# Hybrid decoder layer on one core: the second branch's merge gates made as four seven-product pairs ahead of the recurrence, the attention branch's products moved between its heads

## Chip, core and metric

The program runs on one NeuronCore of one Trainium2 chip, as a single launch. The metric is the device time of one execution in microseconds (us); lower is better. All data are float32. Every large product is made on the tensor engine (PE) from two halves of each operand, a rounded high part and a low remainder, with three matmuls (high by high, high by low, low by high).

## The reference, cut to what matters

One layer over 512 tokens of width 1024: a SwiGLU feed-forward block, a merge of two token mixers, and a second feed-forward block. The change lies in the merge.

```python
u = rms_norm(h, mix_norm_pre[l])
proj = u @ w_in[l]
q, k, v, xr, yr, gl = jnp.split(proj, splits, axis=-1)
...
attn = jnp.einsum('gbsh,gbshe->bshe', alpha, jnp.stack(outs, axis=0).astype(jnp.float32))
attn_d = attn.astype(x.dtype).reshape(B, S, ATTN_OUT_WIDTH) @ w_attn_branch[l]

rec = rg_lru_branch(xr, conv_w[l], conv_b[l], lru_w_x[l], lru_b_x[l],
                    lru_w_a[l], lru_b_a[l], lru_a_param[l]) * jax.nn.gelu(yr)
rec_d = rec @ w_rec_branch[l]

gates = jax.nn.sigmoid(gl).reshape(B, S, N_BRANCHES, D_MODEL)
merged = gates[:, :, 0] * attn_d + gates[:, :, 1] * rec_d
h = h + rms_norm(merged @ w_out[l], mix_norm_post[l])
```

`rg_lru_branch` is a width-4 causal convolution, two gate products per head of 256 channels (four heads), and a linear scan over the 512 tokens.

## The kernel before

Activations stand with the 1024 channels on eight tiles of 128 partitions and the 512 tokens along the row. One "tile" of a product below is 128 output channels by 512 tokens. The code is recorded in program order, and a scheduler then fixes one order of instructions for each engine from priorities (`fetch` and `w_forms` raise the work on weights by 100, PSUM evacuations by 200). On the chip each engine runs its list strictly in that order and waits where an operand or a buffer is not there.

Two ways of making a product matter.

- The plain way, `gemm` (lines L279 to L281 through `mm3`): 24 matmuls of 512 columns for a tile with 1024 input channels, 12 for the attention branch with its 512.
- The seven-product way, `seven` (L639 to L641): two output tiles at once, as a two-by-two block product with seven instead of eight sub-products. Each is 12 matmuls of 256 columns, so a pair is 84 of them. Sums of weight blocks (`w_forms`) and of activation blocks (`forms_of`, names p1 to p7) are formed beforehand.

Weights come as one stream from HBM on SP's queue (`raw_of`, L210), are split into high and low parts by `split` (ACT copies the high part, L264, DVE subtracts the low one, L265), and land in four buffers of 1024 columns (`w8`) or two of 512 (`w4`).

The stretch around the change runs so on PE:

1. the value products, among them `seven512`, which makes two groups of values by seven products (L711 to L713) in the order p1, p2, p6, p7, p4, p5, p3. The activation sums p7 and p5 go into buffers of their own from `big`. The weight blocks u0 come twice into one buffer, `c`, a half of the tile `room`; the other half of it is `first_v`, which sixteen small DMAs on POOL's queue copy elsewhere (L1179);
2. attention for four heads, with the q and k products as twelve pairs between them;
3. four pairs for the first branch's gates (columns 52 to 59 of the stream), with sigmoids into `facc` (L1370, L1371);
4. the eight attention-branch tiles, each multiplied into `facc` by DVE (L1379);
5. the recurrence, a loop over four heads. For head hd it makes two tiles of `branch` (evacuated by DVE, L1443), two of `conv` for the next head (evacuated by ACT, L1427, then the convolution on DVE, L1431), the head's four gate products (`gates_of`, 24 matmuls that read `rec`), and then `recur`, a chain of ACT and DVE work with no PE in it: sigmoid (L1459), tanh (L1470), exp (L1472), a rescale (L1474), then on DVE L1475 to L1477, ACT's square root (L1481), DVE's L1487, L1488, the scan L1489, the product with the gelu branch L1490 and a split into `rec` (L264, L265). Behind `recur` come the second branch's gate tiles that `GATE1` assigns to that head, 0, 2, 2 and 4 of them, made the plain way with a sigmoid out of PSUM (L1505);
6. the eight recurrent-branch tiles, 24 matmuls each, which read all eight tiles of `rec` in order: the last six matmuls of each need the two tiles of the last head.

PSUM has eight banks; in the loop products rotate over four of them and the gate products have the other four. A bank is written again when its earlier content has been read. `h`, needed after stage 6, is fetched back between stages 3 and 4 (L1375).

Of the kernel before, what the change touches and what calls it, by code (L numbers as in the profile page):

```python
# [16 lines left out]
P = 128  # L17
# [23 lines left out]
CB = 6  # L41
GATE1 = ((), (0, 1), (2, 3), (4, 5, 6, 7))

# [25 lines left out]
def stream_plan():  # L69
# [30 lines left out]
    for h in range(NH):  # L100
        qk(h)
    for c in range(0, KC, 2):
        plan.append((("pair", 52 + c, 53 + c), 2048))
    for m in range(KC):
        plan.append((("attn", m), 512))
    for h in range(-1, NH):
        if h >= 0:
            for c in (2 * h, 2 * h + 1):
                plan.append((("in", 44 + c), 1024))
            plan.append((("lru", h), 1024))  # L110
        if h + 1 < NH:
            for c in (2 * h + 2, 2 * h + 3):
                plan.append((("in", 36 + c), 1024))
        if h < 0:
            continue
        for c in GATE1[h]:
            plan.append((("in", 60 + c), 1024))
    for m in range(KC):
# [31 lines left out]
def hybrid_layer(ctx: ExitStack, tc: tile.TileContext, xT: bass.AP, xN: bass.AP, wst: bass.AP,  # L150
# [86 lines left out]
    def big(shape, dt=F32R):  # L237
        return bpool.tile(shape, dt, name="big", tag="b")
# [281 lines left out]

    def forms_of(x, his, los, pool, copied):

# [41 lines left out]
        def fourth():  # L564
            form("p5", big([P, 2, 2, T]), d[1])

# [580 lines left out]
    with ExitStack() as mx:  # L1147
# [66 lines left out]
        vq = [apool.tile([P, T], F32, name="qk", tag="qk", bufs=QKB) for _ in range(4)]  # L1214
        seven512(wbig[0], room[:, 4:8, :].rearrange("q k t -> q (k t)"), vq, v_form, vbank, vy, vz, v_made, v_done)
# [3 lines left out]
        order = [("pair",) + p for ps in pairs for p in ps] + [("pair", 52 + c, 53 + c) for c in range(0, KC, 2)]  # L1219
        forms = {order[0]: w_forms(order[0])}  # L1220

# [144 lines left out]
        for c in range(0, KC, 2):  # L1366
# [3 lines left out]
            ACT.activation(facc[:, c, :], g, AF.Sigmoid)  # L1370
            ACT.activation(facc[:, c + 1, :], u, AF.Sigmoid, scale=-1.0)  # L1371
        apool_cm.__exit__(None, None, None)
        new_h()
        for b in range(4):
            nc.gpsimd.dma_start(hb(b), kept_m[b])  # L1375
        for c in range(KC):
            ps = acc_ps()
            gemm(ps, fetch(("attn", c)), attn)
            DVE.tensor_mul(facc[:, c, :], ps, facc[:, c, :])  # L1379

    with ExitStack() as mx:
        rpool = mx.enter_context(tc.tile_pool(name="rec", bufs=1))
        rec_t = rpool.tile([P, 16, T], F32R, name="rec")
# [111 lines left out]
        for hd in range(NH):  # L1495
# [169 lines left out]
```

## Time and profile before

| | |
|---|---|
| median of three executions | 1230.32 us (1229.68 to 1231.6) |
| the profiled execution | 1229.78 us, of which the span from first to last instruction is 1228.0 us |
| PE busy in the span | 1213.7 us, 99% |
| ACT busy, DVE busy | 740.6 us, 961.2 us |
| granted TensorE clock | 0.998 |
| attention-branch tiles on PE | 615.11 to 636.89 us from the span's start |
| loop over the heads on PE | 636.89 to 791.79 us |
| recurrent-branch tiles on PE | 791.79 to 835.31 us |

Times inside the span are counted from its start. A row of the timeline gives start, duration, engine, line, operation, what is written and read, and in brackets the idle time of the engine before it with what ended it. A PE row's duration is longer than the distance to the next one, since matmuls overlap: the price of a matmul is the distance between starts.

### The profile page before, as it was taken

The page shows a single profiled execution, that of the slowest core. Times are in us where ns is not written, and L with a number is a line of the kernel's source. Part 1 is how long each engine was busy: PE and PEld are TensorE (multiplying, and loading weights), DVE is VectorE, ACT ScalarE, POOL GpSimd, SP SyncE. Part 2 cuts the span into 40 slices and gives each one's busy share as a digit, 9 for nine tenths or more (in the row PEclk, how much of TensorE's full clock was granted, in tenths as well). Part 3 has the DMA queues.
Part 4 walks back from the last instruction along what each step waited for, and adds up shares of the span by engine and source line. Part 5 has one row for each costly group of instructions (what it writes and reads, how often), then busy time and mean ns, then how long its engine had stood idle before and what let it go on. Part 6 is the DMA issues. An engine that isn't in the chain of part 4 may idle for free.

```text
span 1228.0 us, 18986 instructions
## 1 busy us (share of the span) xinstructions
PE 1213.7 (99%) x7556; PEld 1094.4 (89%) x7556; DVE 961.2 (78%) x1504; ACT 740.6 (60%) x1229; POOL 75.6 (6%) x123
## 2 busy tenths in 40 slices
PE   9999999999999999999999999999999999999997
PEld 8898989999878999999988878888899999999996
DVE  7998778988579888888566878655788887979864
ACT  6566665655556564666545878734566665656452
POOL 0001111100102000000000000000110010101000
PEclk9999999999999999999999999999999999999999
DMA  6336646464725322222252222324463555455441
GB/s 245 137 104 172 170 110 175 142 164 119 258 103 166 115 91 91 78 78 104 85 190 73 99 103 69 133 77 166 147 197 104 152 155 153 151 146 159 117 155 69
DMA packets 36025, 163.40 MB, mean 133 GB/s; under 512 B 3936, under 2 KB 7136, under 8 KB 23904
## 3 DMA queue, kind: packets, MB, share of 16 engines
q1 hardware_dynamic: 18288, 107.13, 24.9%
q0 software_dynamic: 17648, 55.06, 17.4%
q8 instruction: 59, 0.97, 0.3%
q14 instruction: 30, 0.25, 0.1%
HBM read 151.69 MB, written 6.29 MB: 129 GB/s over the span
## 4 chain that ended last, share of the span: by engine, by line
PE 84%; DVE 8%; ACT 4%; issue 2%; DMA 2%; SPq 0%; DVEq 0%; ACTq 0%
PE bank L972 9%; PE bank L973 9%; PE bank L974 9%; PE bank L281 5%; PE bank L279 5%; PE bank L280 5%; PE bank L639 4%; PE bank L640 4%; PE bank L641 4%; PE bank L887 4%; PE bank L886 4%; PE bank L888 4%; PE bank L393 3%; PE bank L392 3%; PE bank L394 3%
## 5 line engine op out<-in xcount | busy, mean ns | idle before, releaser
L265 DVE TENSOR_TENSOR w<-raw,w 128x1024 fp32r<-128x1024 f32 (+1 forms) x273 | 295.4, 1093 | 68.7 <-ACT w L264 65.0
L264 ACT ACTIVATE w<-raw 128x1024 fp32r<-128x1024 f32 (+1 forms) x273 | 254.1, 951 | 105.3 <-PE bank L281 50.4
L972 PE MATMUL bank<-big,w 128*128 128x256 f32 x816 | 233.8, 286 | 3.0 <-DVE u L985 1.3
L973 PE MATMUL bank<-big,w 128*128 128x256 f32 x816 | 230.7, 283 | 0.0
L974 PE MATMUL bank<-big,w 128*128 128x256 f32 x816 | 229.4, 283 | 0.0
L972 PEld LDWEIGHTS bank<-big,w 128*128 128x128 f32 x816 | 156.1, 191 | 7.9 <-DVE u L985 2.0
L973 PEld LDWEIGHTS bank<-big,w 128*128 128x128 f32 x816 | 156.2, 191 | 1.6
L974 PEld LDWEIGHTS bank<-big,w 128*128 128x128 f32 x816 | 155.6, 191 | 0.0
L639 PE MATMUL bank<-big,w 128*128 128x256 f32 x320 | 91.8, 287 | 0.0
L640 PE MATMUL bank<-big,w 128*128 128x256 f32 x320 | 91.7, 287 | 0.0
L641 PE MATMUL bank<-big,w 128*128 128x256 f32 x320 | 90.8, 284 | 0.0
L886 PE MATMUL bank<-wd,act 128*128 128x512 f32 x224 | 87.8, 392 | 0.0
L887 PE MATMUL bank<-wd,act 128*128 128x512 f32 x224 | 87.7, 392 | 0.0
L888 PE MATMUL bank<-wd,act 128*128 128x512 f32 x224 | 87.2, 389 | 0.0
L281 PE MATMUL bank<-big,w 128*128 128x512 f32 x192 | 74.8, 390 | 2.1 <-DVE w L265 2.1
L280 PE MATMUL bank<-big,w 128*128 128x512 f32 x192 | 74.7, 389 | 0.0
L279 PE MATMUL bank<-big,w 128*128 128x512 f32 x192 | 74.7, 390 | 0.0
L281 PE MATMUL bank<-act,w 128*128 128x512 f32 (+1 forms) x184 | 64.7, 352 | 0.0
L280 PE MATMUL bank<-act,w 128*128 128x512 f32 (+1 forms) x184 | 64.7, 352 | 0.0
L279 PE MATMUL bank<-act,w 128*128 128x512 f32 (+1 forms) x184 | 64.7, 355 | 0.0
L980 ACT ACTIVATE c<-bank 128x256 f32<-128x256 f32 x70 | 26.6, 381 | 61.2 <-PE bank L974 60.8
L639 PEld LDWEIGHTS bank<-big,w 128*128 128x128 f32 x320 | 61.2, 191 | 1.0
(375 smaller groups left out, 2964.2 us busy)
## 6 DMA issues: line engine op xcount, KB each, us to landing
raw<-in_w SPq DMA_DIRECT2D x90, 1024.0 KB, 4.9
dr<-in_wdn POOLq DMA_DIRECT2D x40, 512.0 KB, 5.4
npair<-in_wdn POOLq DMA_DIRECT2D x32, 512.0 KB, 5.4
big<-act POOLq DMA_DIRECT2D x6, 512.0 KB, 3.2
h<-in_x SPq DMA_DIRECT2D x8, 256.0 KB, 5.2
h<-in_xn POOLq DMA_DIRECT2D x4, 512.0 KB, 5.8
raw<-in_wbig SPq DMA_DIRECT2D x2, 1024.0 KB, 4.7
kept_m<-h POOLq DMA_DIRECT2D x4, 512.0 KB, 2.9
```

Source lines behind the costliest of these rows:

```text
L264: ACT.activation(dh, src, AF.Copy)
L265: DVE.tensor_sub(dl, src, dh.bitcast(F32))
L279: PE.matmul(ps, wh, xh, start=first, stop=False)
L280: PE.matmul(ps, wh, xl, start=False, stop=False)
L281: PE.matmul(ps, wl, xh, start=False, stop=last)
L639: PE.matmul(ps, wh, xh, start=start and k == 0, stop=False, skip_group_check=True)
L640: PE.matmul(ps, wh, xl, start=False, stop=False, skip_group_check=True)
L641: PE.matmul(ps, wl, xh, start=False, stop=k == 3, skip_group_check=True)
L886: PE.matmul(ps, xh, wh, start=start and k == 0, stop=False, skip_group_check=True)
L972: PE.matmul(ps, wh, xh, start=start and k == 0, stop=False, skip_group_check=True)
L973: PE.matmul(ps, wh, xl, start=False, stop=False, skip_group_check=True)
L974: i = PE.matmul(ps, wl, xh, start=False, stop=k == 3, skip_group_check=True)
```

## The change

The second branch's eight gate tiles leave the loop. They are made as four more seven-product pairs directly behind the first branch's four. Their sigmoids are written to a DRAM tile `early` by eight DMAs on POOL's queue, and eight DMAs on the same queue bring them back into `sig` inside the loop. The attention-branch tiles leave their place ahead of the loop and become what stands behind `recur`: 1, 2, 2 and 3 of them. To keep the activation sums p7 and p5 alive longer, they move to the buffers of `first_v` and `c`, and the attention result moves into `big`. The fetch of `h` moves behind the loop.

```diff
-GATE1 = ((), (0, 1), (2, 3), (4, 5, 6, 7))
+EARLY = 8
+FILL = ((('attn', 0),), (('attn', 1), ('attn', 2)), (('attn', 3), ('attn', 4)), (('attn', 5), ('attn', 6), ('attn', 7)))
...
         def second():
             DVE.tensor_sub(x01, x11, x01)
-            form("p7", big([P, 2, 2, T]), x01)
+            form("p7", places["p7"](), x01)
...
         def fourth():
-            form("p5", big([P, 2, 2, T]), d[1])
+            form("p5", places["p5"](), d[1])
...
-        room = tpl.tile([P, 8, T], F32, name="vals", tag="attn")
-        first_v = room[:, 0:4, :]
+        first_v = tpl.tile([P, 4, T], F32, name="vals", tag="v0")
+        third_w = tpl.tile([P, 4, T], F32, name="vals", tag="w3")
...
-        t, steps = forms_of(um, um_t[:2], um_t[2:], apool, False)
+        places = {p: (lambda tag=tag: tpl.tile([P, 2, 2, T], F32R, name="form", tag=tag))
+                  for p, tag in (("p7", "v0"), ("p5", "w3"))}
+        t, steps = forms_of(um, um_t[:2], um_t[2:], apool, False, places)
...
-        attn_t = tpl.tile([P, 8, T], F32R, name="attn", tag="attn")
-        attn = Act([attn_t[:, i, :] for i in range(4)], [attn_t[:, 4 + i, :] for i in range(4)])
+        attn_t = [big([P, 4, T]) for _ in range(2)]
+        attn = Act(*([x[:, i, :] for i in range(4)] for x in attn_t))
...
+        early = dpool.tile([EARLY, P, T], F32, name="early")
+        for c in range(0, EARLY, 2):
+            g, u = tmp("g"), tmp("u")
+            seven(t, pair_of(("pair", 60 + c, 61 + c)), acc_ps()[:, :HB], [g[:, h] for h in HALVES],
+                  [u[:, h] for h in HALVES])
+            ACT.activation(g, g, AF.Sigmoid)
+            ACT.activation(u, u, AF.Sigmoid, scale=-1.0)
+            nc.gpsimd.dma_start(early[c], g)
+            nc.gpsimd.dma_start(early[c + 1], u)
         apool_cm.__exit__(None, None, None)
-        new_h()
-        for b in range(4):
-            nc.gpsimd.dma_start(hb(b), kept_m[b])
-        for c in range(KC):
-            ps = acc_ps()
-            gemm(ps, fetch(("attn", c)), attn)
-            DVE.tensor_mul(facc[:, c, :], ps, facc[:, c, :])
...
             recur(hd, gel, gas, gxs)
-            for c in GATE1[hd]:
+            for c in (2 * hd, 2 * hd + 1):
+                if c < EARLY:
+                    nc.gpsimd.dma_start(sig[:, c, :], early[c])
+            for kind, c in FILL[hd]:
                 ps = acc_ps()
-                gemm(ps, fetch(("in", 60 + c)), um)
-                ACT.activation(sig[:, c, :], ps, AF.Sigmoid)
+                if kind == "attn":
+                    gemm(ps, fetch((kind, c)), attn)
+                    DVE.tensor_mul(facc[:, c, :], ps, facc[:, c, :])
+                else:
+                    gemm(ps, fetch((kind, c)), um)
+                    ACT.activation(sig[:, c - 60, :], ps, AF.Sigmoid)
         lpool_cm.__exit__(None, None, None)
+        new_h()
+        for b in range(4):
+            nc.gpsimd.dma_start(hb(b), kept_m[b])
```

The weight stream is reordered in the same way: four pair blocks of 2048 columns behind the first four, and the attention blocks of 512 between the loop's blocks.

What the scheduler makes of it is shown at three places, all at the end of the loop. The first is DVE in the last head, before: from the third step of the recurrence to the last split into `rec`. `w_` names are weight buffers, `r_` and `th` temporaries, `gt` the gates, `ge` the gelu branch.

```order
L1488 TENSOR_TENSOR gt<-gt,th 128x512
L1487 SCALAR_TENSOR_TENSOR th<-th,r_7238 128x512
L1489 SCALAR_TENSOR_TENSOR th<-gt 128x512
L1488 TENSOR_TENSOR gt<-gt,th 128x512
L1490 TENSOR_TENSOR ge<-th,ge 128x512
L1489 SCALAR_TENSOR_TENSOR th<-gt 128x512
L265 TENSOR_TENSOR w_7425<-raw,w_7425 128x1024
L265 TENSOR_TENSOR rec<-ge,rec 128x512
L1490 TENSOR_TENSOR ge<-th,ge 128x512
L265 TENSOR_TENSOR w_7458<-raw,w_7458 128x1024
L265 TENSOR_TENSOR rec<-ge,rec 128x512
```

The same place in the change; L1514 is the attention tile's product into `facc`, and L264 and L1482 to L1495 are before's L265 and L1477 to L1490:

```order
L1482 TENSOR_TENSOR gt<-th,r_7560 128x512
L1482 TENSOR_TENSOR gt<-th,r_7561 128x512
L264 TENSOR_TENSOR w_7721<-raw,w_7721 128x1024
L1514 TENSOR_TENSOR facc<-bank_76,facc 128x512
L1492 SCALAR_TENSOR_TENSOR th<-th,r_7560 128x512
L1492 SCALAR_TENSOR_TENSOR th<-th,r_7561 128x512
L1493 TENSOR_TENSOR gt<-gt,th 128x512 x2
L1494 SCALAR_TENSOR_TENSOR th<-gt 128x512 x2
L1495 TENSOR_TENSOR ge<-th,ge 128x512 x2
L264 TENSOR_TENSOR w_7754<-raw,w_7754 128x1024
L264 TENSOR_TENSOR rec<-ge,rec 128x512 x2
L1514 TENSOR_TENSOR facc<-bank_73,facc 128x512
```

The two tiles of the last head are now worked side by side, both splits stand at the end, two weight splits and one attention product lie inside the chain, and the last attention product stands behind it.

The second place is ACT at the start of the last head, before:

```order
L1485 ACT_TABLE_LOAD
L1485 ACTIVATE ge<-ge 128x512
L264 ACTIVATE w_7331<-raw 128x1024
L1485 ACTIVATE ge<-ge 128x512
L1459 ACT_TABLE_LOAD
L1459 ACTIVATE gt<-bank_77,first 128x512
L1459 ACTIVATE gt<-bank_78,first 128x512
L1470 ACTIVATE th<-gt,sp_6298 128x512
```

And in the change (L1464 is before's L1459, L1475 its L1470, L1477 its L1472, L263 its L264):

```order
L263 ACTIVATE w_7690<-raw 128x1024
L263 ACTIVATE rec<-ge 128x512
L1464 ACT_TABLE_LOAD
L1464 ACTIVATE gt<-bank_77,first 128x512
L1464 ACTIVATE gt<-bank_78,first 128x512
L1475 ACTIVATE th<-gt,sp_6647 128x512
L1464 ACTIVATE gt<-bank_79,first 128x512
L1475 ACTIVATE th<-gt,sp_6647 128x512
L1464 ACTIVATE gt<-bank_80,first 128x512
L1477 ACT_TABLE_LOAD
L1477 ACTIVATE r_7560<-gt,sp_6648 128x512
L263 ACTIVATE w_7630<-raw 128x512
```

Before, both gelu steps and a weight split lie between the previous head and this one's first sigmoid; now it stands directly behind the previous head's last split into `rec`, and the split of the last attention tile's weights (`w_7630`) stands inside the chain.

The third place is PE behind the last attention tile. The recurrent-branch tiles (`bank_74` is the second of them, `bank_75` the third, `bank_76` the fourth, `bank_73` the first) are begun out of turn: 18 matmuls of the second and 14 of the third stand ahead of these rows.

```order
L278 MATMUL bank_74<-rec,w_7690 128x512
L280 MATMUL bank_75<-rec,w_7721 128x512
L278 MATMUL bank_75<-rec,w_7721 128x512
L279 MATMUL bank_75<-rec,w_7721 128x512
L280 MATMUL bank_75<-rec,w_7721 128x512
L278 MATMUL bank_75<-rec,w_7721 128x512
L278 MATMUL bank_76<-rec,w_7754 128x512
L279 MATMUL bank_74<-rec,w_7690 128x512
L280 MATMUL bank_74<-rec,w_7690 128x512
```

The first of these rows is the 19th matmul of its tile and the first that reads the last head's `rec`. Before, all eight tiles stood whole and in turn behind the four gate tiles of that head. The order of PE ahead of the four added pairs and behind the recurrent-branch tiles is the same in both.

More of the change, by code (lines that the diff above doesn't have):

```diff
@@ L101, in stream_plan @@
         qk(h)
[L102 to L105, printed above, removed]
+    for c in [52 + c for c in range(0, KC, 2)] + [60 + c for c in range(0, EARLY, 2)]:
+        plan.append((("pair", c, c + 1), 2048))
     for h in range(-1, NH):
@@ L115, in stream_plan @@
             continue
-        for c in GATE1[h]:
-            plan.append((("in", 60 + c), 1024))
+        for kind, c in FILL[h]:
+            plan.append(((kind, c), 512 if kind == "attn" else 1024))
     for m in range(KC):
@@ L1214, in hybrid_layer @@
         vq = [apool.tile([P, T], F32, name="qk", tag="qk", bufs=QKB) for _ in range(4)]
[L1215 to L1217 removed]
+        seven512(wbig[0], third_w.rearrange("q k t -> q (k t)"), vq, v_form, vbank, vy, vz, v_made, v_done)
+        attn_t = [big([P, 4, T]) for _ in range(2)]
+        attn = Act(*([x[:, i, :] for i in range(4)] for x in attn_t))
         pairs = [[(g * 4 + hd, 12 + g * 4 + hd) for g in range(NG)] for hd in range(NH)]
         order = [("pair",) + p for ps in pairs for p in ps] + [("pair", 52 + c, 53 + c) for c in range(0, KC, 2)]
+        order += [("pair", 60 + c, 61 + c) for c in range(0, EARLY, 2)]
         forms = {order[0]: w_forms(order[0])}
```

2 lines of the change are left out of this document (1 added, 1 removed).

## Prediction

> **What bounds the kernel now.** I read the page's busy times and its chain of waits first.
>
> ```profile
> span 1228.0 us, 18986 instructions
> PE 1213.7 (99%) x7556; PEld 1094.4 (89%) x7556; DVE 961.2 (78%) x1504; ACT 740.6 (60%) x1229; POOL 75.6 (6%) x123
> PE 84%; DVE 8%; ACT 4%; issue 2%; DMA 2%; SPq 0%; DVEq 0%; ACTq 0%
> ```
>
> PE is the bound: only 1228.0 − 1213.7 = 14.3 us of the span are without a matmul. So the change can gain in two ways, fewer PE cycles or a stall removed, and it can lose through a new stall. Next I went through PE's timeline for distances between starts that are longer than usual, between the value products and the end of the loop. There is one:
>
> ```profile
> 724.33 0.39 PE L280 MATMUL bank<-big,w 128*128 128x512 f32 x1
> 726.83 0.50 PE L281 MATMUL bank<-big,w 128*128 128x512 f32 x1 [2.11 <-DVE w L265]
> 727.16 0.39 PE L279 MATMUL bank<-big,w 128*128 128x512 f32 x1
> ```
>
> The third matmul of a `conv` tile waits for the low part of its weights. At the usual 0.227 us (below) it would start at 724.56 and its successor 0.227 us later: the stall costs 2.27 + 0.10 = 2.4 us. The DVE rows say why it is late:
>
> ```profile
> 724.58 1.06 DVE L1490 TENSOR_TENSOR ge<-th,ge 128x512 f32<-128x512 f32 x1
> 725.55 2.35 DVE L265 TENSOR_TENSOR w<-raw,w 128x1024 fp32r<-128x1024 f32 x2
> ```
>
> The split stands in DVE's list behind the last step of head 1's recurrence.
>
> **Products.** A seven-product pair is 84 matmuls of 256 columns, two plain tiles are 48 of 512. The distances:
>
> ```profile
> 612.23 0.28 PE L639 MATMUL bank<-tx,w 128*128 128x256 f32 x1
> ...
> 613.67 0.28 PE L639 MATMUL bank<-big,w 128*128 128x256 f32 x1
> 615.11 0.40 PE L279 MATMUL bank<-attn,w 128*128 128x512 f32 x1
> 636.89 0.39 PE L279 MATMUL bank<-big,w 128*128 128x512 f32 x1
> ```
>
> Twelve small matmuls take 613.67 − 612.23 = 1.44 us, 0.120 each; the 96 matmuls of the attention tiles take 636.89 − 615.11 = 21.78 us, 0.2269 each. Four pairs: 4 × 84 × 0.120 = 40.32 us. Eight plain tiles: 192 × 0.2269 = 43.56 us. The term is **−3.24 us**. The attention tiles only move. The Trainium skill (TensorE: Matmul & The Clock Gate, "Back-to-back issue gap") gives N/2.4 + 2.5 ns, an estimate of 109 ns for 256 columns and 216 for 512; by it the gain would be 8 × 24 × 0.216 − 336 × 0.109 = 4.8 us. The rows are dearer by the same 11 ns at both lengths, so more matmuls cost more here: 3.24 stands.
>
> **The work beside the pairs.** Each added pair needs weight sums and splits, on DVE and ACT. What the present pairs cost there is in the windows view (sum, then PE, PEld, DVE, ACT, POOL):
>
> ```profile
> 590.40:615.10 24.70, 24.70 (x207) 24.58 (x206) 11.76 (x24) 11.87 (x22) 2.17 (x4) 1.00 0.35 124
> 636.90:791.80 154.90, 152.79 (x674) 125.97 (x673) 113.68 (x147) 121.22 (x155) 0.00 (x0) 1.00 0.27 96
> ```
>
> While PE makes pairs without a gap, DVE and ACT are busy 48% of the time. That is the cover; without it some 20 us of either engine for four pairs would show. Cost 0. The eight DMAs out and the eight back go by POOL's queue, which is idle in the loop (0.00). The ones back are issued ahead of a head's fill tiles and are read first in stage 6, ten or more us later; `h` is fetched later, but needed only there too. Cost 0.
>
> **The stall at 724 us.** G0 to G3 are the ends of the four heads' gate products on PE; the rows below are the first matmuls behind G2 = 742.83, G3 = 770.03 and G1 = 702.35, and the first DVE step of head 1's recurrence:
>
> ```profile
> 742.83 0.39 PE L279 MATMUL bank<-big,w 128*128 128x512 f32 x1
> 770.03 0.39 PE L279 MATMUL bank<-big,w 128*128 128x512 f32 x1
> 702.35 0.39 PE L279 MATMUL bank<-big,w 128*128 128x512 f32 x1
> 711.36 0.69 DVE L1475 SCALAR_TENSOR_TENSOR gt<-th,r 128x512 f32<-128x512 f32 x1 [3.60 <-ACT r L1474]
> ```
>
> In the change DVE's list has that split behind the fifth step of head 1's recurrence instead of behind its end. The first step starts at 711.36 − 702.35 = 9.0 us behind G1; five steps of 0.6 and two splits later it is about 14.3. The conv tile now follows two attention tiles (5.44) and two branch tiles (10.88), G1 + 16.3. The stall goes: **−2.4 us** (bounds −2.4 and 0). What is late next is the bank of the second conv tile: it was read last by an attention product that stands on DVE behind this recurrence, by my count 0.5 us after PE wants it: **+0.5** (0 to 1.5).
>
> **The end of the loop** carries the largest risk. Before, four gate tiles of 5.44 us hid the last recurrence:
>
> ```profile
> 791.79 0.39 PE L279 MATMUL bank<-rec,w 128*128 128x512 f32 x1
> 792.09 0.69 DVE L265 TENSOR_TENSOR rec<-ge,rec 128x512 fp32r<-128x512 f32 x1
> ```
>
> The last split ends at 792.09 + 0.69 = 792.78, 22.75 us behind G3; PE begins the recurrent tiles 21.8 us behind G3 and reads that split still later. Now three attention tiles stand there, 36 × 0.2269 = 8.2 us, then 32 matmuls of recurrent tiles that need only the first six tiles of `rec`, 7.3 us. So PE has 15.5 us of cover for a chain of about 22. I worked the chain out from G2, since with less work between them two recurrences stand in series:
>
> ```profile
> 682.72 1.29 DVE L1475 SCALAR_TENSOR_TENSOR gt<-th,r 128x512 f32<-128x512 f32 x2 [1.24 <-ACT r L1474]
> ...
> 686.35 1.22 DVE L265 TENSOR_TENSOR w<-raw,w 128x1024 fp32r<-128x1024 f32 x1
> ...
> 688.08 1.29 DVE L1487 SCALAR_TENSOR_TENSOR th<-th,r 128x512 f32<-128x512 f32 x2
> ...
> 690.50 2.33 DVE L1489 TENSOR_TENSOR_SCAN th<-gt 128x512 f32<-128x512 f32 x2
> ...
> 694.71 1.21 DVE L265 TENSOR_TENSOR w<-raw,w 128x1024 fp32r<-128x1024 f32 x1
> 695.84 1.28 DVE L265 TENSOR_TENSOR rec<-ge,rec 128x512 fp32r<-128x512 f32 x2
> 697.04 0.74 DVE L1431 SCALAR_TENSOR_TENSOR sig<-xr,first,sig 128x512 f32<-128x512 f32 x1
> 749.46 0.69 DVE L1475 SCALAR_TENSOR_TENSOR gt<-th,r 128x512 f32<-128x512 f32 x1 [3.58 <-ACT r L1474]
> 768.08 1.28 ACT L1459 ACT_TABLE_LOAD   x1
> 769.37 1.26 ACT L1459 ACTIVATE gt<-bank,first 128x512 f32<-128x512 f32 x2
> ...
> 776.09 1.05 ACT L264 ACTIVATE w<-raw 128x1024 fp32r<-128x1024 f32 x1
> 376.24 4.62 DVE L265 TENSOR_TENSOR w<-raw,w 128x1024 fp32r<-128x1024 f32 x4
> ```
>
> DVE's own part, without other work in between, is (686.35 − 682.72) + (690.50 − 688.08) + (694.71 − 690.50) + (697.04 − 695.84) = 11.46 us. A weight split of 1024 columns is 1.14 (4.62 / 4), a step of 512 is 0.6. ACT's part, from the table load to its last step ahead of DVE's first, is 776.09 − 768.08 = 8.0, and 0.55 more for the half split `w_7630` that now stands in it: 8.55.
>
> Head 2, behind G2: DVE's first step at 7.5 (749.46 gives 6.6; I add 0.9 since ACT comes later from head 1), plus 11.46, plus 3.5 for two splits of 512, two copies and one of 1024: its last split ends at 22.5, ACT's at 20.7. Head 3: ACT starts behind that, 20.7 + 8.55 = 29.3. Then DVE's 11.46, two splits 2.28, one attention product 0.6: last `rec` complete at 43.6, the high part of its first tile 2.7 before, at 40.9. PE behind G2: two attention tiles 5.44, two branch tiles 10.88, gate products 5.44, three attention tiles 8.16, 32 matmuls 7.26: it wants that first tile at 37.2. Three waits: about 1.0 at the last attention tile (its weight split stands in ACT's chain), then 40.9 − 38.2 = 2.7 at the 19th matmul, and 0.5 for the low part: **+4.2 us**. The low bound is head 3's chain as before from its own gates, with two of its four weight splits gone: 22.75 − 2.28 = 20.5, its first high part 2.7 earlier at 17.8, so 17.8 − 15.5 + 0.5 = 2.8. The high bound is the second rival's.
>
> **The value stage.** x-p5 now lies in buffer `c`, so its split stands behind both splits of w-p5, whose second source comes from SP at
>
> ```profile
> 392.38 0.33 SPq L679 DMA_DIRECT2D vals<-in_wbig  x1
> 397.19 2.50 DVE L702 TENSOR_TENSOR vals<-vals,qk 128x512 f32<-128x512 f32 x4
> 404.42 0.39 PE L711 MATMUL bank<-w,big 128*128 128x512 f32 x1
> ```
>
> From the adds' end at 399.7 to the product there are 4.7 us for two 1024-splits on each engine, 2.3, and the form's own sum and split, 2.3. It just fits: +0.1 (0 to 1.2). x-p7's buffer is free in time: `first_v`'s last DMAs were issued by
>
> ```profile
> 380.04 1.96 POOL L1179 DMA_DIRECT2D vals<-vals  x4 [0.37 <-issue]
> ```
>
> while x-p7 is split near 384.6: 0. DVE's four splits at 376.24 run beside them at the usual 1.14, so POOL's DMAs do not slow DVE.
>
> **Sum:** −3.24 − 2.4 + 0.5 + 4.2 + 0.1 = −0.8 us. Made against the profiled 1229.78 that is 1229.0; the median of the runs lies 0.54 above that execution, so I forecast **1229.5**, no difference that can be told: 0.2% here is 2.46 us, so below 1227.86 is faster and above 1232.78 slower.
>
> **Rivals.**
>
> *The end is covered (faster).* If the two recurrences overlap as before, ACT starting head 3 while DVE still works on head 2, the waits fall from 4.2 to the bound's 2.8, 1228.1, and towards nothing, 1229.5 − 4.2 = 1225.3, if the chain itself is shorter too. It decides from waits under 2.5 us; midway it gives 1226.7. For it: DVE has 154.9 − 113.68 = 41 us free in the loop, and ACT loses its sigmoids there. Against it: the order of ACT puts head 3's first sigmoid directly behind head 2's last split, and PE's cover is 15.5 us against a DVE part alone of 14.3.
>
> *Two recurrences in series (slower).* One mechanism, in heads 2 and 3: each takes as long as long as before's longest ones. Head 1's last split ended at 727.82 + 0.69 = 728.51, 26.2 us behind G1:
>
> ```profile
> 727.82 0.69 DVE L265 TENSOR_TENSOR rec<-ge,rec 128x512 fp32r<-128x512 f32 x1
> ```
>
> Add the last head's 22.75 and `rec` is complete 48.9 us behind G2 instead of 43.6: 5.3 more, **1234.8**. It decides slower once the chain ends later than 43.6 + 3.3 = 46.9. For it: both were stretched by weight splits inside the chain, and the change's order has such splits too; ACT is busy 121 of 154.9 us. Against it: ACT's sigmoids of eight gate tiles and their table loads leave the loop, and head 0 with the same steps is short.
>
> *Table loads.* A change of function set on ACT, four to a recurrence, may cost more than its row. By the row 768.08 + 1.28 = 769.36 the next instruction starts at once, so nothing is hidden. The Trainium skill (ScalarE: Activation LUTs, "What ACT_TABLE_LOAD costs") adds a drain of about 1.38 us to each load; by it four of them in the exposed chain would be an estimate of 5.5 us more, 1235. The trace does not agree.
>
> *The gates do not gain.* If the added pairs starve for weight sums, −3.24 goes and some us come: 1233 or more. The window of the present pairs, at 48%, speaks against it.
>
> **Chances.** The forecast, waits of 3 to 6 us, 0.57; end covered 0.23; series 0.16; table loads 0.02; starved pairs 0.02. The range leaves out the far part of the first two rivals: 1226.6 to 1233.4. Faster is the covered end (0.23) and a little of the forecast's edge, 0.24; slower is the other three, 0.20; within 0.2%: 0.56.
>
> **What would show it.** Right: attention tiles gone from 615 us and pairs of 10.1 us each in their place; no gap in front of the conv tile of head 2; PE idle for 3 to 5 us at the end of the loop, ended by ACT's or DVE's `rec`; DVE's last split 43 to 44 us behind G2. Wrong: a gap at a pair that a weight sum ends, a gap near 404 us ended by the split into `c`, PE idle in a branch or conv tile, or a last split earlier than 40 or later than 47.

## The result: slower by 0.18%

The changed kernel takes 1232.58 us (median of 19 runs, 1231.66 to 1234.99), the kernel before, beside it, 1230.64 (19 runs, 1229.54 to 1231.83). The ratio is 1.0018, with a 95% interval of 1.0011 to 1.0024. The forecast was 1229.5 and no difference; the change is slower, by 1.9 us between the medians.

The profile after, in the same order of views. The page's span, busy times and chain of waits:

```profile
span 1230.3 us, 19405 instructions
PE 1213.9 (99%) x7700; PEld 1099.9 (89%) x7700; DVE 983.6 (80%) x1544; ACT 745.8 (61%) x1248; POOL 84.3 (7%) x139
PE 84%; DVE 8%; ACT 5%; issue 2%; DMA 0%; DVEq 0%; ACTq 0%
```

PE is the bound as before and is busy about as long (1213.9 us against 1213.7), although eight plain tiles became four pairs. So what the pairs saved was eaten by something that counts as busy, and the span grew by 2.3 us. PE's timeline gives the marks: the first added pair, the first matmul of the loop, the wait in head 2, the first and the last of the attention tiles behind head 3 (the last behind a wait), the first recurrent-branch matmul, the first reader of the last head's `rec`, and the end of the recurrent-branch tiles.

```profile
615.41 0.28 PE L638 MATMUL bank<-big,w 128*128 128x256 f32 x1
...
656.41 0.40 PE L278 MATMUL bank<-big,w 128*128 128x512 f32 x1
...
745.97 0.39 PE L280 MATMUL bank<-big,w 128*128 128x512 f32 x1
747.94 0.47 PE L278 MATMUL bank<-big,w 128*128 128x512 f32 x1 [1.58 <-ACT rec L263]
...
780.66 0.39 PE L278 MATMUL bank<-big,w 128*128 128x512 f32 x1
...
785.88 0.39 PE L280 MATMUL bank<-big,w 128*128 128x512 f32 x1
786.80 0.50 PE L278 MATMUL bank<-big,w 128*128 128x512 f32 x1 [0.54 <-ACT w L263]
...
789.93 0.39 PE L278 MATMUL bank<-rec,w 128*128 128x512 f32 x1
...
796.96 0.39 PE L279 MATMUL bank<-rec,w 128*128 128x512 f32 x1
799.70 0.50 PE L278 MATMUL bank<-rec,w 128*128 128x512 f32 x1 [2.35 <-ACT rec L263]
...
837.69 0.39 PE L391 MATMUL bank<-w,big 128*128 128x512 f32 x1
```

Read as distances at the usual spacing of 0.2269 us:

| step | forecast | measured, and from which rows |
|---|---|---|
| PE ahead of the added pairs | +0.1 | +0.3: 615.41 against 615.11 |
| four pairs for eight plain tiles | −3.24 | −2.56: 656.41 − 615.41 = 41.00, less 43.56 |
| stall in front of a conv tile of head 2 | −2.4 | −2.4: no such gap is left |
| bank of the second conv tile | +0.5 | +1.74: 747.94 − 745.97 = 1.97, less 0.23 |
| the three attention tiles behind head 3 (0.69 of it the wait) | +1.0 | +1.1: 789.93 − 780.66 = 9.27, less 8.17 |
| the recurrent-branch tiles | +3.2 | +4.2: 837.69 − 789.93 = 47.76, less 43.56 |
| sum | −0.8 | +2.4; PE ends this stretch at 837.69 instead of 835.31 |

The last step is more than its wait. The wait costs 799.70 − 796.96 − 0.23 = 2.51 us, and 1.7 of the 4.2 are left. They stand in the rows behind the wait, and in the windows view, whose last but two column is the granted clock:

```profile
800.57 0.63 PE L279 MATMUL bank<-rec,w 128*128 128x512 f32 x1
801.00 0.63 PE L280 MATMUL bank<-rec,w 128*128 128x512 f32 x1
...
803.56 0.51 PE L279 MATMUL bank<-rec,w 128*128 128x512 f32 x1
803.91 0.40 PE L280 MATMUL bank<-rec,w 128*128 128x512 f32 x1
...
799.70:800.50 0.80, 0.80 (x3) 0.68 (x4) 0.80 (x2) 0.44 (x1) 0.00 (x0) 0.93 0.00 0
802.00:803.00 1.00, 1.00 (x4) 0.81 (x3) 0.90 (x2) 0.00 (x0) 0.00 (x0) 0.50 0.00 0
804.00:806.00 2.00, 2.00 (x11) 1.64 (x10) 1.62 (x3) 1.27 (x2) 0.00 (x0) 1.00 0.00 0
```

From 800.4 to 803.8 us the granted clock is 0.50, and matmuls of 512 columns start 0.427 us apart instead of 0.227. PE counts as busy in that time: this is part of how PE's busy time kept its length. Behind the stall of the kernel before (2.11 us idle) there is nothing of the kind; the window 728 to 729 there has a clock of 1.00:

```profile
728.00:729.00 1.00, 1.00 (x6) 0.80 (x5) 1.00 (x2) 0.00 (x0) 0.00 (x0) 1.00 0.58 197
```

Nor do all runs of the change have it. Four of the 19 have a mean granted clock of 1.000, where 3.4 us at one half would leave 0.9986; they took 1231.83 to 1232.10 us. So the half clock is part of the profiled execution's time, but the change is slower than the kernel before (1230.64) without it too. By the table, +2.4 less 1.7 leaves +0.7.

The chain that sets the end is the one that the prediction worked out. Its steps in the change, on ACT (head 3's table load and first sigmoids) and DVE (its first step, and the last split into `rec`); the gates of head 2 end at 758.90 here:

```profile
779.25 1.28 ACT L1464 ACT_TABLE_LOAD   x1
780.55 1.27 ACT L1464 ACTIVATE gt<-bank,first 128x512 f32<-128x512 f32 x2
787.91 1.29 DVE L1480 SCALAR_TENSOR_TENSOR gt<-th,r 128x512 f32<-128x512 f32 x2 [0.44 <-ACT r L1479]
801.01 1.29 DVE L264 TENSOR_TENSOR rec<-ge,rec 128x512 fp32r<-128x512 f32 x2
```

The load, DVE's first step and the end of the split (802.30) lie 20.4, 29.0 and 43.4 us behind those gates; forecast were 20.7, 29.3 and 43.6.

### The profile page after: what moved, and what is told of

It reads as the page before. It is cut to its first block, busy times and chain, and to the rows that moved or that the text cites. A ratio compares the mean times of both kernels' runs of the same rounds, so it can differ in the third digit from the quotient of the medians.

```text
span 1230.3 us, 19405 instructions
## 1 busy us (share of the span) xinstructions
PE 1213.9 (99%) x7700; PEld 1099.9 (89%) x7700; DVE 983.6 (80%) x1544; ACT 745.8 (61%) x1248; POOL 84.3 (7%) x139
## 4 chain that ended last, share of the span: by engine, by line
PE 84%; DVE 8%; ACT 5%; issue 2%; DMA 0%; DVEq 0%; ACTq 0%
PE bank L971 9%; PE bank L972 9%; PE bank L973 9%; PE bank L638 6%; PE bank L639 5%; PE bank L640 5%; PE bank L278 5%; PE bank L280 5%; PE bank L279 5%; PE bank L886 4%; PE bank L885 4%; PE bank L887 4%; PE bank L393 3%; PE bank L392 3%; PE bank L391 3%; DVE w L264 2%
## 5 line engine op out<-in xcount | busy, mean ns | idle before, releaser
L264 DVE TENSOR_TENSOR w<-raw,w 128x1024 fp32r<-128x1024 f32 (+1 forms) x277 | 297.9, 1087 | 67.2 <-ACT w L263 61.5
L263 ACT ACTIVATE w<-raw 128x1024 fp32r<-128x1024 f32 (+1 forms) x277 | 256.1, 946 | 89.6 <-PE bank L280 29.5
L971 PE MATMUL bank<-big,w 128*128 128x256 f32 x816 | 233.8, 287 | 3.0 <-DVE u L984 1.3
L972 PE MATMUL bank<-big,w 128*128 128x256 f32 x816 | 230.7, 283 | 0.0
L973 PE MATMUL bank<-big,w 128*128 128x256 f32 x816 | 229.4, 283 | 0.0
L971 PEld LDWEIGHTS bank<-big,w 128*128 128x128 f32 x816 | 156.2, 191 | 7.9 <-DVE u L984 1.9
L972 PEld LDWEIGHTS bank<-big,w 128*128 128x128 f32 x816 | 156.3, 192 | 1.6
L973 PEld LDWEIGHTS bank<-big,w 128*128 128x128 f32 x816 | 155.7, 192 | 0.0
L638 PE MATMUL bank<-big,w 128*128 128x256 f32 x240 | 69.6, 290 | 0.0
L640 PE MATMUL bank<-big,w 128*128 128x256 f32 x240 | 68.2, 284 | 0.0
L639 PE MATMUL bank<-big,w 128*128 128x256 f32 x240 | 67.9, 283 | 0.0
L278 PE MATMUL bank<-big,w 128*128 128x512 f32 x160 | 62.5, 390 | 2.1 <-ACT rec L263 1.6
L280 PE MATMUL bank<-big,w 128*128 128x512 f32 x160 | 62.4, 390 | 0.0
L279 PE MATMUL bank<-big,w 128*128 128x512 f32 x160 | 62.3, 389 | 0.0
L264 DVE TENSOR_TENSOR wd<-npair,wd 128x1024 fp32r<-128x1024 f32 x24 | 29.3, 1223 | 39.2 <-ACT wd L263 39.2
```

The lines of the kernel that those rows point to most:

```text
L263: ACT.activation(dh, src, AF.Copy)
L264: DVE.tensor_sub(dl, src, dh.bitcast(F32))
L278: PE.matmul(ps, wh, xh, start=first, stop=False)
L279: PE.matmul(ps, wh, xl, start=False, stop=False)
L280: PE.matmul(ps, wl, xh, start=False, stop=last)
L638: PE.matmul(ps, wh, xh, start=start and k == 0, stop=False, skip_group_check=True)
```

## Experiments

The theory after the result: the loss is made of a bank wait in head 2, a weight wait at the last attention tile, a wait for the last `rec`, and a clock that falls to half after that wait; the added pairs themselves cost nothing else. All ratios are against the kernel before, run beside it on the same chip; "the change" is 1232.58 us. Edits of `FILL` are given in short: the number of attention tiles behind each of the four recurrences.

**e1: fill the idle time.** Eleven matmuls that nobody reads, behind the last attention tile.

```diff
+        spare = aux_ps()
+        for i in range(11):
+            PE.matmul(spare, attn.hi[0][:, 0:P], attn.hi[1], start=i == 0, stop=i == 10)
+        turns["aux"] -= 1
```

> Eleven matmuls of 512 columns whose result nobody reads (attention operands, into a gate bank) are put on PE behind the last attention tile, 2.5 us of work in front of the place where PE stood idle for 2.35 us; nothing else is changed. Theory (the idle time drops the granted clock to half for some 3.3 us, which costs 1.7 us beyond the wait itself): the idle time is filled, the clock stays at 1.0, the matmuls behind it stand 0.227 us apart, and the time falls by 1.7 less at most 0.2: about 1231.0. Rival (the matmuls at 0.427 us are slow because of what DVE does to the freshly written rec, not because of idle time): they stay slow, 1232.6 to 1232.8.

1235.23 us, ratio 1.0034 (1.0021 to 1.0047). Both expectations missed, because the idle time was not filled: the scheduler, which counts the eleven as work, put only 21 instead of 32 recurrent-branch matmuls ahead of the first one that waits. PE stood idle as long as in the change, at the same time, and ran slow behind it:

```profile
797.08 0.39 PE L280 MATMUL bank<-rec,w 128*128 128x512 f32 x1
799.82 1.72 PE L278 MATMUL bank<-rec,w 128*128 128x512 f32 x3 [2.36 <-ACT rec L263]
```

The time grew by 2.65 us between the medians (2.0 by the ratios), about the eleven matmuls (2.5). That PE's order is fixed ahead by the scheduler's own idea of time is what this run taught; e9 uses it.

**e2: evacuate the attention products early.**

```diff
-                    DVE.tensor_mul(facc[:, c, :], ps, facc[:, c, :])
+                    with tc.high_priority(offset=EVAC):
+                        DVE.tensor_mul(facc[:, c, :], ps, facc[:, c, :])
```

> Only the priority of the attention products into facc is raised to that of the other evacuations, so that DVE's list has them ahead of the recurrences and the bank of the second attention tile is free early. Theory (the 1.7 us gap in front of the second conv tile of head 3 is that bank): the gap goes, the last chain is at most 0.6 us later for the product moved into it, the end stays as it is: 1230.9 to 1231.6. Rival (the wait there is for ACT's split into rec, as the row names it, or what is saved there comes back as a longer wait at the end, since the recurrences follow each other in series): gap unchanged, or gone with an end wait longer by as much: 1232.6.

1234.75 us, 1.0032 (1.0019 to 1.0044). The gap in front of head 2's second conv tile is gone, so it was the bank. The row of the change names ACT's split into `rec` as its end; DVE's product into `facc` ended just before it, at 747.80, and PE started at 747.94:

```profile
747.10 0.70 DVE L1514 TENSOR_TENSOR facc<-bank,facc 128x512 f32<-128x512 f32 x1
```

But the time rose: ACT's list was different too, a weight split in it waited for its transfer ahead of the split into `rec`, and the last attention tile's weights came behind the whole of ACT's start of the recurrence:

```profile
780.47 1.06 ACT L263 ACTIVATE w<-raw 128x1024 fp32r<-128x1024 f32 x1 [1.59 <-DMA raw<-in_w]
781.43 0.61 ACT L263 ACTIVATE rec<-ge 128x512 fp32r<-128x512 f32 x1
...
788.94 0.61 ACT L263 ACTIVATE w<-raw 128x512 fp32r<-128x512 f32 x1
...
789.61 0.79 PE L278 MATMUL bank<-big,w 128*128 128x512 f32 x1 [4.95 <-ACT w L263]
790.20 0.63 PE L279 MATMUL bank<-big,w 128*128 128x512 f32 x1
```

PE waited 4.95 us for the weights and then ran at 0.427 again, here in an attention tile that has nothing to do with `rec`.

**e3 and e4: more attention tiles behind the last head.** Two ways of placing the tiles behind the four recurrences instead of 1, 2, 2, 3.

```diff
-FILL: 1, 2, 2, 3 attention tiles
+FILL: 0, 2, 0, 6 (e3)
+FILL: 0, 0, 0, 8 (e4)
```

> The attention tiles stand behind the recurrences as 0, 2, 0, 6 instead of 1, 2, 2, 3. Theory (the loss is cover: the last recurrence ends 43.4 us behind the gates of head 2, and PE has 16.3 us of branch and gate products, now 16.3 of attention tiles and 7.3 of early matmuls, 39.9, instead of 37.2): the end wait falls from 2.5 to some 0.8 us or less, no half clock, no bank wait (both attention products of head 1 stand ahead of the recurrence in DVE's list): 1232.6 - 1.7 - 0.7 - 1.7 - 1.7 = 1226.8, between 1226 and 1228. Rival (the loss lies in the added pairs and their weights, or in the moved activation sums, not in the loop): 1231.5 or more.

> All eight attention tiles stand behind the last recurrence. Theory: 45.4 us of PE work behind the gates of head 2 against a chain of 43.4: no wait at the end. What is late next is the weight split of a conv tile behind heads 0 and 1, which now follows the gate products after 10.9 us while the split stands in DVE's list inside the recurrence, some 12 us behind them: 1 to 3 us. So 1232.6 - 1.7 - 0.7 - 2.5 - 1.7 + 1 to 3 = 1227 to 1229. Rival (only the number of attention tiles behind the last two heads counts, and nothing is late in heads 0 and 1): 1226.0. Rival (the loss is not in the loop): 1231.5 or more.

e3: 1232.83 us, 1.0018 (1.0009 to 1.0027). e4: 1238.72 us, 1.0066 (1.0054 to 1.0079). Neither theory holds; e3's time is the one that its rival gave, but the loss does lie in the loop. The wait for the last `rec` did fall (to 0.28 us of idle PE in e3), but a larger one came in its place, for attention weights: 3.38 us in e3 at the third of the six tiles, 5.72 in e4 at the third of the eight. In e4 another 2.81 us follow at the first recurrent-branch tile, for a bank. The row of e4, and ACT's before it:

```profile
776.66 0.72 ACT L1477 ACTIVATE r<-gt,sp 128x512 f32<-128x512 f32 x1
777.29 0.61 ACT L263 ACTIVATE w<-raw 128x512 fp32r<-128x512 f32 x1
...
777.95 0.80 PE L278 MATMUL bank<-big,w 128*128 128x512 f32 x1 [5.72 <-ACT w L263]
```

There are two buffers for weights of 512 columns. The third tile's weights can be split only when the first tile is done, and by then ACT's list is inside the last recurrence. An attention tile is poor cover for a recurrence: its weights need the engine that it is to cover.

**e5 and e6: four buffers for the attention weights**, with the tiles as in the change (e5) and as in e3 (e6).

```diff
+        def slot_of(c):
+            return (w4 if c % 4 < 2 else lambda: lpool.tile([P, 2, 512], F32R, name="wa", tag="wa", bufs=2)), AHEAD
...
-                    gemm(ps, fetch((kind, c)), attn)
+                    gemm(ps, held[c] if c in held else fetch((kind, c), *slot_of(c)), attn)
```

(`held` stays empty. Three small constants of the recurrence share tiles in both runs, to make room.)

> The change with four buffers instead of two for the 512-column weights of the attention tiles (three small constants of the recurrence share tiles to make room); tiles behind the recurrences as in the change. Theory (with two buffers the weights of the last attention tile can only be split once an earlier tile is done, and by then ACT's list is inside the last recurrence, where the split delays both): no wait at the last attention tile (0.7 + 0.2 us), ACT's part of the last chain 0.5 shorter; the wait for the last rec stays near 2.5 us with its half clock: 1231 to 1232. Rival (buffers do not matter, the end is set by the chain alone): 1232.6.

> Four buffers for the attention weights and the tiles placed 0, 2, 0, 6. With two buffers this placing waited 3.4 us for ACT's copy of the weights of the third of the six tiles and then ran at half clock. Theory (buffers of the attention weights, then cover): the weight wait and the half clock behind it (3.5 + 0.4 + 1.4 us) go, what stays is under 1 us at a conv tile and under 1.5 at the end: 1227 to 1229. Rival (the order of ACT's list only shifts the same wait to another weight or to the chain): 1231 or more.

e5: 1235.38 us, 1.0036 (1.0023 to 1.0049). e6: 1236.4 us, 1.0039 (1.0025 to 1.0053). The waits at attention tiles went in both, as the theory had it, and the sum did not follow. In e5 ACT began head 3 at 782.62 instead of 779.25 (1.1 of it since the whole execution lay later at the pairs already), and a gelu step of head 2 ahead of it waited 1.33 us for DVE's copy; the split into `rec` came 2.8 us later (801.84 against 799.01) and PE, after 31 matmuls, waited 5.13 us:

```profile
780.98 0.63 ACT L1490 ACTIVATE ge<-ge 128x512 f32<-128x512 f32 x1 [1.33 <-DVE ge L1448]
...
797.00 0.39 PE L278 MATMUL bank<-rec,w 128*128 128x512 f32 x1
802.52 0.79 PE L278 MATMUL bank<-rec,w 128*128 128x512 f32 x1 [5.13 <-ACT rec L263]
```

In e6 it waited 1.92 and 4.73 us for the weights of the recurrent-branch tiles. e6's rival holds, the repair moved the wait along the fixed lists; e5 came out above both of its expectations, and in the same way.

**e7: half of the change.** `EARLY = 4`: four gate tiles as two pairs; the other four plain behind the last head, as before; four attention tiles ahead of the loop, two each behind heads 1 and 2.

```diff
-EARLY = 8
+EARLY = 4
-FILL: attention 1, 2, 2, 3
+FILL: attention 0, 2, 2, 0 (four ahead of the loop); gate tiles 64 to 67 behind head 3
```

> Only four of the gate tiles are made as two early pairs; the other four stand plain behind the last recurrence as before, four attention tiles stay ahead of the loop, two each go behind heads 1 and 2. Theory (what the change lost is the cover of the last recurrence, 21.8 us of gate tiles whose weights have four buffers): no wait at the end and no half clock; the products gain half, 21.8 - 20.6 = 1.2; the stall of 2.4 us in front of head 2's conv tile goes or is replaced by up to 1.7 (a bank): 1230.5 - 1.2 - 2.4 + 0 to 1.7 = 1227 to 1228.6. Rival (the early pairs themselves or the moved sums cost something that is not seen in the loop): 1230 or more.

1228.73 us, 0.9983 (0.9973 to 0.9992): faster than both, 0.1 us above what the theory gave. The recurrent-branch tiles take 43.5 us, no wait in them; a wait of 0.94 us in head 2 is left.

**e8: the added pairs alone.** The attention tiles stay ahead of the loop; nothing stands behind a recurrence.

> The four added pairs alone: the attention tiles stay ahead of the loop, nothing stands behind a recurrence. Theory (the tiles behind the last recurrence are its cover): behind the last gate products PE has only 32 early matmuls, 7.3 us, against a chain of some 22 us whose first high part comes 2.7 us before its end: a wait of 12 us at the end, the half clock behind it 2 us, and a wait of 1 to 5 us in front of a conv tile of a middle head: 1230.5 - 2.4 - 2.4 + 15 to 19 = 1241 to 1245. Rival (ACT and DVE, freed of the attention tiles' weights in the loop, finish the chains much earlier, and the tiles were no cover worth having): under 1236.

1234.48 us, 1.0028 (1.0016 to 1.0039). The theory, which had three attention tiles for the cover, is wrong by 6.5 us and more; the rival is right in size, though not in its reason: the chain ended 42.8 us behind G2 (814.48 − 771.71), 43.4 in the change. PE did have cover: with no attention tile there, the scheduler put 72 matmuls of four recurrent-branch tiles ahead of the first reader of the last head, 16.3 us instead of the change's 32 and 7.3 us. The last head's `rec` was in time; the waits left, 3.18 and 1.14 us, are for head 2's. So what the change lost at the end was not only the gate tiles: with three attention tiles (8.2 us) behind the last head, the scheduler also put 9 us of early matmuls behind the first one that waits. That it did so for want of banks is argued, not shown; on the chip the banks allow both, as e9 shows, which keeps the three tiles.

**e9: the early matmuls first.** The change, with the first six input tiles of four recurrent-branch tiles ahead of the last two.

```diff
+        ahead, wr = [acc_ps() for _ in range(4)], [fetch(("rec", c)) for c in range(4)]
+        for lo, hi in ((0, 6), (6, 8)):
+            for ps, wt in zip(ahead, wr):
+                for k in range(lo, hi):
+                    mm3(ps, k128(wt[0])[:, k, :], k128(wt[1])[:, k, :], rec.hi[k], rec.lo[k], k == 0, k == 7)
...
```

> The change, with the first four recurrent-branch tiles written so that their 72 matmuls on the first six tiles of rec (16.3 us) all stand ahead of the first one that reads the last head; before, 32 did. Theory (the 2.35 us of idle PE and the half clock behind it come from PE's fixed order: matmuls that could run stand behind one that waits): the wait for the last rec goes and the half clock with it, 2.5 + 1.7 us; the bank wait of 1.7 in head 2 and the 0.9 at the last attention tile stay: about 1228.4, between 1227.5 and 1229.5. Rival (four weights at once must be split inside the last recurrence, so the wait moves to a weight or a bank): 1231 or more.

1230.21 us, 0.9988 (0.9979 to 0.9998). The wait for the last `rec` is gone and the half clock with it. The same stretch as above, in windows, and the first and last rows of the recurrent-branch tiles:

```profile
797.00:805.00 8.00, 8.00 (x37) 6.63 (x36) 5.82 (x7) 1.27 (x2) 0.00 (x0) 1.00 0.00 1
...
791.04 0.39 PE L278 MATMUL bank<-rec,w 128*128 128x512 f32 x1
...
835.00 0.39 PE L391 MATMUL bank<-w,big 128*128 128x512 f32 x1
```

835.00 − 791.04 = 43.96 us against 47.76 in the change and 43.56 without any wait. 0.9 us of the 3.8 came back at the last attention tile, whose weight wait grew to 1.6 us (a split of 1024 columns more stands ahead of it on ACT): about half of the miss from 1228.4 by the medians.

**e10 and e11: the repairs together.** e10 is e5, e2 and e9 in one; e11 is all eight gates early, four attention tiles ahead of the loop, two behind each of the last two heads (FILL 0, 0, 2, 2), with the edits of e2 and e9.

```diff
+FILL: 1, 2, 2, 3, four buffers, early evacuation, 72 matmuls first (e10)
+FILL: four ahead, 0, 0, 2, 2, early evacuation, 72 matmuls first (e11)
```

> The change's own placing of tiles with three repairs together: four buffers for the attention weights, the attention products evacuated at the priority of other evacuations, and the 72 early matmuls. Theory (the losses are these three and the half clock): 1232.6 - 0.9 - 1.7 - 4.2 = 1225.8, between 1225 and 1227.5. Rival (in-order lists of ACT and DVE: repairs placed inside the last recurrence delay it as in the two runs that had one of them alone, which were slower than the change): 1230 or more.

> All eight gate tiles as early pairs, four attention tiles back ahead of the loop, two behind each of the last two recurrences, evacuated at the priority of other evacuations, and the 72 early matmuls. Theory (cover from the gates of head 2 on: two attention tiles 5.4, branch and gates 16.3, two attention tiles 5.4, early matmuls 16.3, together 43.4 us against some 41 to the first high part of the last rec): no wait at the end, no half clock; gaps of up to 1 us in the middle: 1230.5 - 2.4 - 2.4 + 0 to 1 = 1225.7 to 1227. Rival (heads 0 and 1 without tiles behind them make the conv tiles wait for DVE as before): 1228 to 1230.

e10: 1232.31 us, 1.0006 (0.9996 to 1.0015). e11: 1236.38 us, 1.0033 (1.002 to 1.0047), above both of its expectations. The wait for `rec` stayed away in both, and a bank took its place: a recurrent-branch tile needs the bank of the last attention tile, and DVE's product that frees it now stands inside the recurrence, behind steps that wait for ACT. In e11:

```profile
789.35 0.39 PE L282 MATMUL bank<-rec,w 128*128 128x512 f32 x1
797.60 0.79 PE L280 MATMUL bank<-rec,w 128*128 128x512 f32 x1 [7.86 <-DVE facc L1521]
...
796.25 0.69 DVE L1486 SCALAR_TENSOR_TENSOR gt<-th,r 128x512 f32<-128x512 f32 x1 [1.31 <-ACT r L1485]
796.86 0.68 DVE L1521 TENSOR_TENSOR facc<-bank,facc 128x512 f32<-128x512 f32 x1
```

**e12: what the runs point to.** No attention tile behind the last head: six gates early, two plain behind head 3, the matmuls of e9 first.

```diff
-EARLY = 8
+EARLY = 6
-FILL: attention 1, 2, 2, 3
+FILL: attention 0, 2, 2, 0 (four ahead of the loop); gate tiles 66 and 67 behind head 3; 72 matmuls first
```

> Six gate tiles as three early pairs, two plain behind the last recurrence; four attention tiles ahead of the loop, two each behind heads 1 and 2, none behind head 3; the 72 early matmuls of the recurrent-branch tiles ahead of the first reader of the last head. Theory (what stands behind the last recurrence must neither need attention weights split nor a bank freed inside it; cover 10.9 of gate tiles and 16.3 of early matmuls is enough for 22): no wait at the end over 0.5 us, products gain 3/4 of 2.4 = 1.8, the 2.4 us stall replaced by about 1: 1231 - 1.8 - 1.4 = 1227.8, between 1226.5 and 1229. Rival (the plain gate tiles' sigmoids stand on ACT inside the recurrence and hold the banks of the third and fourth recurrent tile, as the attention products did): 1230 or more.

1227.68 us, 0.9973 (0.9963 to 0.9983), as expected (1227.8), and the fastest of all. The recurrent-branch tiles take 832.99 − 789.47 = 43.52 us, no wait in them; of the loop's waits one is left:

```profile
745.11 0.39 PE L281 MATMUL bank<-big,w 128*128 128x512 f32 x1
746.27 0.50 PE L282 MATMUL bank<-big,w 128*128 128x512 f32 x1 [0.77 <-DVE w L266]
...
789.47 0.39 PE L280 MATMUL bank<-rec,w 128*128 128x512 f32 x1
...
832.99 0.39 PE L393 MATMUL bank<-w,big 128*128 128x512 f32 x1
```

## Why the prediction was wrong

The forecast said −0.8 us in the profiled execution, and it was +2.3. The forecast waits were there; the sum is off by 3.2 us, 3.0 of it in three of its terms, all to the same side. One cost had no term, and two terms were mis-sized.

- **The end of the loop, "+4.2 us".** The chain was right to 0.3 us at each of its marks, and the waits that were summed (1.0, 2.7 and 0.5) were measured as 1.1 and 2.5, so 3.6 against 4.2. What the step left out is that a wait of this length can cost more than its length: in the profiled execution 1.7 us of half clock stand behind it. e9 shows that they hang on the wait: without it, the matmuls at the same place on the same operands run at full clock. Runs without the half clock (four of 19, see above) still lie 2.3 us and more above the forecast, so the two terms below weigh as much.
- **The bank, "+0.5 (0 to 1.5)".** The mechanism was right, as e2 shows; the size was 1.74, beyond the bound. DVE's product ended 23.4 us behind G1 (747.80 − 724.44) where 22.3 was counted, with three weight splits of 1024 columns inside head 1's recurrence on DVE; that is 1.1 of the miss, and 0.14 is the way from its end to PE's start.
- **The products, "−3.24 us".** A pair was priced at 84 × 0.120 from a stretch of twelve matmuls. From pair to pair it takes 10.25 us, not 10.08: two distances in each are longer, 0.20 and 0.22. The trace of before has both: its third pair of gates takes 605.03 − 594.78 = 10.25 us, the fourth 615.11 − 605.03 = 10.08. The first of the longer distances stands ahead of the matmul that starts a pair's second product. By the code (`seven`, five banks in turn) that product writes the bank which DVE's last add of the pair before (L650) reads, and in all four added pairs it starts 0.05 us behind the end of that add. In the change, 606.21 + 0.42 = 606.63:

```profile
606.21 0.42 DVE L650 TENSOR_TENSOR g<-bank,c 128x256 f32<-128x256 f32 x1
...
606.48 0.28 PE L640 MATMUL bank<-big,w 128*128 128x256 f32 x1
606.68 0.39 PE L638 MATMUL bank<-big,w 128*128 128x256 f32 x1
606.90 0.28 PE L639 MATMUL bank<-big,w 128*128 128x256 f32 x1
```

In the last pair of before, that add comes 0.2 us behind the pair's start instead of 1.05, directly behind PE's last product, and nothing is late:

```profile
605.23 0.42 DVE L651 TENSOR_TENSOR g<-bank,c 128x256 f32<-128x256 f32 x1 [1.00 <-PE bank L641]
```

So the pairs were priced without a wait for a bank. No run moved this add.

- **The stall at 724 us, "−2.4 us"**, went as forecast. **The value stage, "+0.1"**: some 0.3 us at 615 us, of which 0.13 stands ahead of the gate pairs; within what two executions differ by. **Weight sums of the added pairs, 0**: no gap of the change is ended by one. **The DMAs to and from `early`, 0**: none ends a gap of PE.
- **The rivals.** "The end is covered" fell: only e7, e9 and e12 have the recurrent-branch tiles without a wait. "Two recurrences in series" has the right side for a wrong reason: the chain ended 43.4 us behind G2, not 48.9. The table loads cost their row (ACT's next step starts at 780.55, 1.30 behind the load at 779.25). No rival had the clock.
- One step of the reasoning, right in the sum, was wrong as a picture: the three attention tiles as PE's cover. e8, without any, is little slower than the change (ratios 1.0028 and 1.0018, some 1.2 us). The reason is put together from other runs and was not tried alone: the tiles take weights through ACT (the waits of e2, e3 and e4) and free their banks through DVE (e10, e11) inside the chain that they are to cover.

What stays open: the second of the two longer distances of a pair, and how much of the slower runs e2, e5 and e6 goes to each of the moved steps in ACT's and DVE's lists.

## What to carry to other kernels

Price a stretch that is to be repeated by its distance from one repetition to the next, not by the spacing inside it, and not by the last repetition alone. Work that is to cover a chain must not need that chain's engines, neither to prepare its operands nor to free its banks; and where the engines run fixed lists, first look whether the reader itself has work that does not yet wait (here 72 matmuls), and write it ahead of the part that does. A wait of PE above some 2 us is to be priced with the slow matmuls that may follow it, here 1.7 us for one stretch at half clock.

## What the runs showed of the hardware

The clock's fall was not expected at this length. Eleven times in these runs PE stood idle for 2.35 us or longer in or behind the loop (2.35, 2.36, 2.81, 3.18, 3.38, 3.82, 4.73, 4.95, 5.13, 5.72, 7.86 us), at attention tiles and at recurrent-branch tiles, and each time the granted clock fell to 0.50 and matmuls of 512 columns ran 0.427 us apart (in e8 the clock fell at 796.3, 1.2 us behind the end of the 3.18). It stayed there for 3.41 us (the change, e1, e3, the second fall of e4), 6.83 (e2, e4, e5, e6, e8, e10) or 10.24 (e11), some of it while PE still stood idle: one, two or three times the same length.

The changes of the clock keep to a grid of that length. In the change it falls at 800.39 and, behind the last matmul, at 1227.06: 125 times 3.413 us. So it matters where an idle time lies in the grid. The 2.35 us of the change lie whole between two edges (796.98 and 800.39). In the kernel before the clock falls at 1224.07, behind the last matmul; counted back from there, an edge at 725.7 divides the stall of 2.11 us (724.72 to 726.83) into 1.0 and 1.1, and the clock stayed at 1.00. Between two edges, 2.2 us of idle PE were enough for a fall (e8, 792.89 to 796.30), and 1.9 were not (e6, 787.86 to 791.27). This reading is worked out from the traces, no run was made to try it; by it the same wait costs its length alone in executions where an edge divides it, which agrees with the four runs at a clock of 1.000.

The Trainium skill (TensorE: Matmul & The Clock Gate, "What's actually happening") gives half rate after an idle window of about 3.4 us and full rate after about as long a busy one. The length agrees with the 3.41 us here. For the fall to half rate, 2.2 us of idle time within one such stretch were enough, and the measurement decides.
